# Two window tiles of the sample attention in other places, and their first loads on another queue

## The chip, the cores and the metric

The kernel runs on one core of one Trainium2 chip. Its time is the device time of one execution in microseconds (us); the profile is of one execution too. Five engines work side by side, each in its own order: PE (matrix products, and turning tiles over through a product with the identity; PEld is its weight load), DVE (vector operations, and 32x32 block transposes), ACT (activations and copies), POOL (element-wise work, and requests to transfer data) and SP (requests only). Transfers (DMA) go between the large memory and the on-chip memory of 128 partitions, SBUF. PE writes its results to eight accumulator banks, PSUM, from which DVE and ACT fetch them.

## The reference

One inference step of a decoder layer for a prompt of 512 tokens and eight sample sequences of eight tokens, each of these with 2048 cached tokens. Two attentions stand beside each other: FoX, over all tokens with a forgetting bias, and NSA, with three parts (compressed blocks, selected blocks, a window of 512). Then gates, an output projection and an MLP follow. What matters here is the sample sequences' attention:

```python
fox_all = jnp.concatenate([gather_pages(fox_pool, page_table), pm['fox_rows']], axis=1)
o_fox = fox_attend(pm['fox_q'], cf[:, past:], pos[past:], fox_all[:, :, 0], fox_all[:, :, 1], cf, pos)
nsa_all = jnp.concatenate([gather_pages(nsa_pool, page_table), pm['nsa_rows']], axis=1)
win_all = jnp.concatenate([win_buf, pm['win_rows']], axis=1)
o_nsa = nsa_attend(pm['nsa_q'], pos[past:], pm['nsa_gate'], kc, vc, c_end, ks_blk, vs_blk,
                   win_all[:, :, 0], win_all[:, :, 1], w_pos)
```

For each sequence 2 MB of FoX rows, 2 MB of selected-block rows and 512 KB of window rows are read.

## The kernel before, in words

**Stages.** A first stage sums the compressed blocks; then come projections, the prompt's attention (until about 427 us), the sample sequences' attention (about 422 to 545), the mixing of the branches with the output projection, and the MLP.

**The sample stage** (`sample_attention`) walks the eight sequences b = 0 to 7. Three pairs of rooms, each room 16 KB per partition, hold the rows in turn: `fr` for FoX and `sr` for the selected blocks. Pair 0 (fr0, sr0) and pair 1 (fr1, sr1) are tiles of their own; pair 2 lies in `room2`, which the prompt's attention uses until its end. A piece is a quarter of a room; `sample_fox(b, i, eng)` asks for FoX piece i of sequence b in one transfer of 512 KB, `sample_page(b, i, eng)` for the NSA piece in four transfers of 128 KB, one per page, whose numbers the queue first loads from the page table (L162). All go through `dma` (L151), which fixes their order on the queue as written. Window rows come in one transfer of 512 KB per sequence into `wr0` (even b) or `wr1` (odd b), by `window_load` (L1615).

For each sequence, PE forms scores (`ss`, L77, from rows that DVE has turned in `key_turn`, L1809), the last of them from two small tiles, `W2` and `CT`, which ACT fills by copies. DVE adds a ramp and takes the maxima (L1828, into `zF`; for the new tokens L1843, and L1851 for the new tokens of the window), ACT takes exponentials of `sN` and `zF`, PE turns them (`spn`, then sixteen `sp`), ACT copies these to `spT` and `zK`, and PE multiplies them with the rows (`so`). Only when `so` has read a piece may the next sequence but two be loaded there. The window goes by pairs of sequences: `window_keys` (L1908) turns wr's keys on PE (`wk`) and ACT copies them to `wkt`; `window_scores` (`sw`) uses both tiles of a pair. For the first pair, `window_keys(0)` and `window_keys(1)` stand ahead of `turn_weights(0)`, so that PE's order is wk of sequence 0, wk of sequence 1, spn, sp, so, sw, ss of sequence 1.

**What sets the order.** PE's order is the order of the program here (`link`, L87, chains each product to the one before). For the other engines a planner, which runs the program against its own idea of the times, sets the order unless `issue_after` fixes it. Requests of SP and POOL take eight semaphores each in turn, so a queue issues a transfer only when the one eight before it on that queue has landed.

**Places in SBUF.** Pools are opened and closed like a stack. A tile takes the bytes that follow the tile before it, and at its first write waits for the last use of each earlier tile that had any of these bytes. The pool `spw` lies over the prompt stage's buffers. Per partition, from its start:

| tile | bytes | what lay there in the prompt stage, latest first |
|---|---|---|
| D3b | 0 to 2047 | factors of the last FoX heads (Ffox3, ffox3) |
| CT | 2048 to 4095 | ffox3, Ffox1 |
| W2 | 4096 to 8191 | ffox2, Ffox1, early tiles |
| wr0 | 8192 to 12287 | compressed-block tiles cS, cP, cT |
| wkt, two tiles | 12288 to 16383 | cT, PTfox300, PTfox310 |
| wr1 | 16384 to 20479 | PTfox310, PTfox302, PTfox301 |

The buffers of the prompt stage there are: one of 2048 bytes that ends at 895 (Ffox3), one from 896 (ffox3), two from 2944 on (Ffox1, then ffox2), cpos, triS and first cS (7040 to 9087), later cS, cP and cT (to 13183), and four of 2048 from 13184 on (PTfox300, PTfox310, PTfox302, PTfox301). PTfox are turned weights of the last prompt heads, which PE reads in its last `ofox` products; Ffox1 is read by DVE in `oT<-ofox,Ffox` of the second FoX head, ffox2 by PE in `fcfox` of the third.

**Requests ahead of the loop** (L1650 to L1663): SP asks in the written order for sequence 1, with wr0 ahead of FoX piece 3, and then for sequence 2. POOL copies a part of D3b (L1657), prepares keys of sequence 1 (`key_prep`), asks for pages 0 and 2 of sequence 2, then for wr1, and prepares keys of sequence 2.

Of the kernel before, what the change touches and what calls it, by code (L numbers as in the profile page):

```python
# [6 lines left out]
F32 = mybir.dt.float32  # L7
# [7 lines left out]
P = 128  # L15
# [30 lines left out]
class Step:  # L46
# [1573 lines left out]
    def sample_attention(self, sp, ctx):  # L1620
# [11 lines left out]
        maps = [t(f"map{x}", [P, n]) for x, n in enumerate((2, 2, 2, 4))]  # L1632
        pw = self.pool("spw", ctx)
        self.D3.append(pw.tile([P, 16, 32], F32, name="D3b"))
        self.CT = pw.tile([P, 512], F32R, name="CT")
        self.W2 = pw.tile([P, NB, P], F32R, name="W2")
        w0 = pw.tile([P, 4, 256], F32, name="wr0")
        self.wkt = [pw.tile([P, 512], F32, name=f"wkt{x}") for x in range(2)]
        self.wrt = [w0, pw.tile([P, 4, 256], F32, name="wr1")]
        for b in range(3):  # L1640
            self.rows[b] = self.rooms[b]
        self.chain = ""
# [5 lines left out]
            self.key_counts(0)  # L1648
            self.act(self.CT, self.ct)
        page, fox = self.sample_page, self.sample_fox  # L1650
        for ask, b, i in ((fox, 1, 0), (fox, 1, 1), (page, 1, 0), (fox, 1, 2), (page, 1, 1), (fox, 1, 3), (page, 1, 2), (fox, 2, 0),
                          (page, 1, 3), (fox, 2, 1), (fox, 2, 2), (fox, 2, 3), (page, 2, 1), (page, 2, 3)):
            if (b, i) == (1, 3) and ask == fox:
                self.window_load(0, "sync")
            ask(b, i, "sync")
        with self.tc.issue_after(self.issued["gpsimd"]):
            self.nc.gpsimd.tensor_copy(self.D3[1][:, :, 16:32], self.D3[0][:, :, 16:32])  # L1657
        self.key_prep(1)
        for i in (0, 2):
            page(2, i, "gpsimd")  # L1660
        self.window_load(1, "gpsimd")
        self.key_prep(2)
        last = NB - 1  # L1663

# [1074 lines left out]
```

## Time and profile before

| what | us |
|---|---|
| median of three runs | 1149.46 (1149.41 to 1152.69) |
| the profiled execution | 1152.17 |
| its span, first to last instruction | 1150.5 |
| PE busy in the span | 1086.0 |
| DVE busy | 821.0 |
| ACT busy | 544.5 |
| POOL busy | 230.5 |

Times in the views count from the span's start. In a timeline row stand the start, the length, the engine (PEld is the weight load, SPq the queue of SP), the line of the kernel, the operation, output and inputs by the names of the program (without numbers), sizes, and in brackets the idle time before it with what ended it; "issue" is a wait for nothing that the profile shows. Neighbours that are alike are merged to one row with a count. A row of the windows view has: the stretch, its length, the busy time of PE, PEld, DVE, ACT and POOL with their numbers of instructions, the granted clock of PE as a share, the busy share of the DMA engines, and GB/s. A row of the waits view has the waiting engine and operation, who ended the wait, and the total, the number and the longest of these waits.

### The profile page before, as it was taken

What the parts mean: (1) busy time and instruction counts of PE and PEld (TensorE: products, weight loads), DVE (VectorE), ACT (ScalarE), POOL (GpSimd) and SP (SyncE); (2) the same over time, 40 slices, a digit from 0 to 9 for tenths busy, and PEclk for the clock granted to TensorE, in tenths of its full rate; (3) what the DMA queues carried; (4) which work ended last, traced back from release to release, by engine and by line L of the source; (5) the groups of instructions that cost most, each with busy time, mean ns of one, the idle gap of its engine ahead of it and who ended that gap; (6) DMA issues with size and microseconds to landing.
All of it is one profiled execution on the core that took longest, in us unless ns stands there. A gap on an engine that the chain in (4) does not pass through costs nothing.

```text
span 1150.5 us, 24616 instructions
## 1 busy us (share of the span) xinstructions
PE 1086.0 (94%) x9089; PEld 937.6 (81%) x9089; DVE 821.0 (71%) x2011; ACT 544.5 (47%) x1146; POOL 230.5 (20%) x320
## 2 busy tenths in 40 slices
PE   3899999999999995789999999999999999999998
PEld 3897789988666654556999999998989989899896
DVE  5898666685788865766987757769657658475668
ACT  3466643444777754456644435372514324143230
POOL 6540000002211513441000000012312122321202
PEclk9899999999999997999999999999999999999999
DMA  8997585764786797996643364252313224132242
GB/s 197 294 287 212 195 275 149 246 215 135 254 269 208 214 283 229 349 337 197 179 103 86 88 196 126 72 169 72 111 37 111 74 73 140 44 111 69 61 118 84
DMA packets 169049, 191.75 MB, mean 167 GB/s; under 512 B 17849, under 2 KB 147330, under 8 KB 166754
## 3 DMA queue, kind: packets, MB, share of 16 engines
q1 hardware_dynamic: 154674, 151.52, 44.7%
q0 software_dynamic: 12080, 37.62, 9.9%
q8 instruction: 71, 1.16, 0.4%
q10 hardware_dynamic: 2176, 1.05, 0.4%
q14 instruction: 48, 0.39, 0.1%
HBM read 179.89 MB, written 31.16 MB: 183 GB/s over the span
## 4 chain that ended last, share of the span: by engine, by line
PE 80%; DVE 7%; DMA 5%; ACT 3%; issue 3%; SPq 2%; POOL 0%; POOLq 0%; DVEq 0%; ACTq 0%
PE dn L77 18%; PE hid L77 6%; PE z L77 5%; PE br L77 4%; PE wo L77 4%; PE up L77 4%; PE upx L77 3%; PE upv L77 3%; DMA winr<-in_w_in 3%; PE mg L77 2%; PE ss L77 2%; SPq L155 2%; PE so L77 2%; PE mgv L77 2%; PE mgx L77 2%
## 5 line engine op out<-in xcount | busy, mean ns | idle before, releaser
L100 DVE TENSOR_TENSOR acc<-acc,dn 128x512 f32<-128x512 f32 x66 | 44.3, 684 | 54.0 <-PE dn L77 53.9
L77 PE MATMUL hid<-xh,w1hlk 128*128 128x256 f32 (+1 forms) x192 | 47.6, 341 | 16.8 <-ACT xh L112 16.8
L77 PE MATMUL z<-winh,h2r 128*128 128x264 f32 (+1 forms) x288 | 57.3, 288 | 2.3 <-ACT adw L112 2.3
L77 PE MATMUL z<-winh,h 128*128 128x264 f32 (+1 forms) x288 | 55.8, 284 | 0.0
L112 ACT ACTIVATE xh<-cpg 128x512 fp32r<-128x512 f32 x64 | 37.6, 623 | 36.2 <-PE hid L77 22.3
L112 ACT ACTIVATE u<-c 128x512 fp32r<-128x512 f32 x64 | 24.1, 434 | 59.2 <-PE dn L77 45.3
L77 PE MATMUL hid<-xh,w1hlv 128*128 128x256 f32 (+1 forms) x192 | 47.9, 341 | 3.9 <-ACT w1hlv L112 2.4
L131 DVE TENSOR_TENSOR xl<-cpg,xh 128x512 fp32r<-128x512 f32 x64 | 42.3, 682 | 11.6 <-ACT xh L112 11.5
L77 PEld LDWEIGHTS hid<-xh,w1hlk 128*128 128x128 f32 x192 | 33.3, 202 | 20.7 <-ACT xh L112 17.0
L2403 POOL TENSOR_TENSOR wur<-wur 128x512 f32<-128x512 f32 x12 | 19.8, 1653 | 148.4 <-DVE wu1l L131 55.5
L77 PEld LDWEIGHTS z<-winh,h2r 128*128 128x128 f32 x288 | 45.6, 190 | 3.6 <-ACT adw L112 2.5
L77 PEld LDWEIGHTS z<-winh,h 128*128 128x128 f32 x288 | 45.8, 190 | 0.0
L77 PE MATMUL z<-winl,h 128*128 128x264 f32 (+1 forms) x160 | 44.5, 284 | 0.5 <-DVE winl L131 0.5
L470 DVE STREAM_TRANSPOSE cpg<-cpg 128x1024 f32<-128x1024 f32 (+1 forms) x36 | 39.2, 1109 | 7.3 <-DMA cpg<-in_cache_nsa_kv 7.2
L77 PE MATMUL z<-winl,h2r 128*128 128x264 f32 (+1 forms) x160 | 44.4, 284 | 0.0
L155 POOL DMA_DIRECT2D cpg<-in_cache_nsa_kv x72 | 37.7, 525 | 27.9 <-issue 12.3
L77 PEld LDWEIGHTS hid<-xh,w1hlv 128*128 128x128 f32 x192 | 33.6, 202 | 8.0 <-ACT w1hlv L112 2.6
L77 PE MATMUL br<-oL,wbh 128*128 128x288 f32 x128 | 37.7, 295 | 0.0
L77 PE MATMUL br<-oH,wbl 128*128 128x288 f32 x128 | 37.7, 295 | 0.0
L77 PE MATMUL br<-oH,wbh 128*128 128x288 f32 x128 | 37.7, 294 | 0.0
L1828 DVE CUSTOM_DVE_ANT_1 zF<-ss,scr 128x512 f32<-128x512 f32 x32 | 20.2, 687 | 20.5 <-PE ss L77 20.5
L131 DVE TENSOR_TENSOR winl<-winr,winh 128x1056 fp32r<-128x1056 f32 (+1 forms) x16 | 19.6, 1234 | 18.7 <-ACT winh L112 18.6
(926 smaller groups left out, 3605.2 us busy)
## 6 DMA issues: line engine op xcount, KB each, us to landing
adw<-in_w_ada SPq DMA_DIRECT2D x16, 1024.0 KB
foxD<-in_cache_fox_kv SPq DMA_DIRECT2D x128, 128.0 KB
wur<-in_w_up SPq DMA_DIRECT2D x32, 512.0 KB
wdr<-in_w_down SPq DMA_DIRECT2D x32, 512.0 KB
wada<-in_w_ada SPq DMA_DIRECT2D x8, 1024.0 KB
sr<-in_cache_nsa_kv SPq DMA_DIRECT2D x64, 128.0 KB
cpg<-in_cache_nsa_kv SPq DMA_DIRECT2D x56, 128.0 KB
cpg<-in_cache_nsa_kv POOLq DMA_DIRECT2D x56, 128.0 KB, 5.7
```

Of the source, the lines that this page charges most:

```text
L77: ins = self.nc.tensor.matmul(out, a, b, start=start, stop=stop, skip_group_check=True)
L100: self.nc.vector.tensor_tensor(out, a, b, op=op)
L112: return self.nc.scalar.activation(out, in_, f, **kw)
L131: self.splits.append((eng or self.nc.vector).tensor_tensor(l, x, h.bitcast(F32), op=OP.subtract).ins)
L155: self.issued[eng] = getattr(self.nc, eng).dma_start(out, in_).ins
L470: self.flipped = self.nc.vector.transpose(v, v).ins
L1828: self.nc.vector.tensor_tensor_reduce(self.S[:, :, q, :], pbs[q].rearrange("p (c s) -> p c s", s=32), self.ramp[:, None, 32 * (q % 2):32 * ...
L2403: gp(a12, a12, a11, op=OP.subtract)
```

## The change

The two window tiles get other places in the pool, `wr1` behind an unused tile `edge` of 896 bytes; the other tiles of the pool shift with them. And both first window loads are asked for by SP: sequence 0's ahead of FoX piece 0 of sequence 1, and sequence 1's ahead of FoX piece 2, which now also stands ahead of page piece 0. POOL's request for wr1 is gone.

```diff
         self.D3.append(pw.tile([P, 16, 32], F32, name="D3b"))
+        pw.tile([P, 224], F32, name="edge")
+        w1 = pw.tile([P, 4, 256], F32, name="wr1")
         self.CT = pw.tile([P, 512], F32R, name="CT")
+        self.wrt = [pw.tile([P, 4, 256], F32, name="wr0"), w1]
         self.W2 = pw.tile([P, NB, P], F32R, name="W2")
-        w0 = pw.tile([P, 4, 256], F32, name="wr0")
         self.wkt = [pw.tile([P, 512], F32, name=f"wkt{x}") for x in range(2)]
-        self.wrt = [w0, pw.tile([P, 4, 256], F32, name="wr1")]
...
-        for ask, b, i in ((fox, 1, 0), (fox, 1, 1), (page, 1, 0), (fox, 1, 2), (page, 1, 1), (fox, 1, 3), (page, 1, 2), (fox, 2, 0),
+        for ask, b, i in ((fox, 1, 0), (fox, 1, 1), (fox, 1, 2), (page, 1, 0), (page, 1, 1), (fox, 1, 3), (page, 1, 2), (fox, 2, 0),
                           (page, 1, 3), (fox, 2, 1), (fox, 2, 2), (fox, 2, 3), (page, 2, 1), (page, 2, 3)):
-            if (b, i) == (1, 3) and ask == fox:
-                self.window_load(0, "sync")
+            if b == 1 and ask == fox and i in (0, 2):
+                self.window_load(i // 2, "sync")
             ask(b, i, "sync")
...
             page(2, i, "gpsimd")
-        self.window_load(1, "gpsimd")
         self.key_prep(2)
```

By the same stack of bytes the places after the change are:

| tile | bytes | what lay there in the prompt stage |
|---|---|---|
| D3b | 0 to 2047 | as before |
| edge | 2048 to 2943 | (never written) |
| wr1 | 2944 to 7039 | Ffox1, ffox2 |
| CT | 7040 to 9087 | cpos, triS, cS |
| wr0 | 9088 to 13183 | cS, cP, cT |
| W2 | 13184 to 17279 | PTfox300, PTfox310 |
| wkt, two tiles | 17280 to 21375 | PTfox302, PTfox301 |

## Prediction

> **What bounds the kernel now.** I read the views from the whole to the stage: page, chain of waits, windows, then one engine at a time around the longest wait.
>
> ```profile
> span 1150.5 us, 24616 instructions
> PE 80%; DVE 7%; DMA 5%; ACT 3%; issue 3%; SPq 2%; POOL 0%; POOLq 0%; DVEq 0%; ACTq 0%
> ```
>
> PE sets the end; what is not PE on the chain is where time can come from. The chain of waits over the start of the sample stage, in order of time (start, length, what):
>
> ```profile
> 425.36 1.45 PE ofox L77 x8
> ...
> 426.91 0.70 DVE oT L100
> ...
> 427.73 0.40 POOL D3b L1657
> ...
> 429.51 5.17 DMA room<-in_cache_nsa_kv
> ...
> 437.02 6.02 DMA wr<-in_state_win_kv
> 443.03 0.14 issue
> 443.17 1.09 PE wk L83 x4
> 444.26 0.21 PE spn L83
> 444.47 3.33 PE sp L83 x16
> 447.81 1.03 PE so L77 x64
> ```
>
> The chain leaves PE at 426.8, goes through DVE's last prompt product to POOL's D3b (L1657), POOL's eight page requests for sequence 2, and only then to wr1, the second sequence's window rows (L1661), which land at 443.03. PE and ACT, with the stage's rows by window:
>
> ```profile
> 429.78 0.66 PE L83 MATMUL wk<-identF,wr 128*128 128x128 f32 x4
> 443.17 1.09 PE L83 MATMUL wk<-identF,wr 128*128 128x128 f32 x4 [12.74 <-DMA wr<-in_state_win_kv]
> ```
> ```profile
> 435.00:440.00 5.00, 0.00 (x0) 0.00 (x0) 3.05 (x7) 0.84 (x3) 1.28 (x3) 0.50 1.06 356
> 442.00:449.50 7.50, 6.33 (x89) 5.45 (x89) 0.00 (x0) 3.66 (x7) 0.57 (x1) 0.63 0.06 15
> 450.00:470.00 20.00, 16.48 (x434) 10.15 (x419) 16.83 (x63) 9.27 (x21) 11.00 (x22) 1.00 0.97 333
> ```
>
> The reader is to see three things. PE turned wr0's keys at 429.78 and then stood 12.74 us for wr1, with nothing else to do, since its order is written out. Its clock (third column from the right) fell to 0.50. And the transfers (share, last but one) were full until about 442, empty to 449.5, and full again: the idle PE held back the rooms into which sequence 3's rows go.
>
> **The change, part by part.** It has three: places, requests on SP, one request less on POOL.
>
> *Places.* The tiles of the old stage are laid one behind the other, so the sizes in the code give who lay there. wr1 moves from the room of PTfox302, PTfox301 and the end of PTfox310 (read by PE until 426.8, the 425.36 row) to that of Ffox1 and ffox2 exactly, the `edge` tile of 896 bytes being what makes it exact. wr0 goes over cS, cP and cT buffers; CT over cpos, triS and cS; W2 over PTfox300 and PTfox310; wkt, first written behind 430, over PTfox302 and PTfox301. The last uses:
>
> ```profile
> 411.92 0.61 PE L83 MATMUL fcfox<-identF,ffox 128*128 128x128 f32 x4
> 423.32 1.07 PE L77 MATMUL ofox<-PTfox,zK 128*64 128x512 f32 x4
> 428.96 0.51 PE L77 MATMUL ss<-CT,W 32*128 32x512 f32 x4
> ```
> ```profile
> 410.42 0.69 DVE L100 TENSOR_TENSOR oT<-ofox,Ffox 128x512 f32<-128x512 f32 x1
> ```
> ```profile
> L77 PE MATMUL oc<-cT,pvc x16: 587/613/638, 298.8 to 360.6; 32*64 32x512 f32 x16
> ```
>
> wr1's new place is free at 412.5 (411.92 + 0.61; Ffox1 at 411.1), wr0's since about 361. W2 is the one tile that gets a later release: 423.32 + 1.07 = 424.4. ACT's copies to W2 and CT:
>
> ```profile
> 422.65 1.06 ACT L112 ACTIVATE W<-scr 128x1024 fp32r<-128x1024 f32 x1
> 423.60 0.63 ACT L112 ACTIVATE CT<-oT 128x512 fp32r<-128x512 f32 x1
> 432.66 0.35 ACT L112 ACTIVATE sN<-sN,ss 128x64 f32<-128x64 f32 x1 [8.43 <-DVE ss L1858]
> 434.14 1.13 ACT L112 ACTIVATE zF<-zF,ss 128x1024 f32<-128x1024 f32 x1
> 435.27 0.57 ACT L112 ACTIVATE wkt<-wk 128x512 f32<-128x512 f32 x1
> 444.36 0.60 ACT L112 ACTIVATE wkt<-wk 128x512 f32<-128x512 f32 x1 [8.51 <-PE wk L83]
> ```
>
> W2 then ends at 425.5 and CT, queued behind it, at 426.1; PE wants both at 428.96, and ACT has nothing else before 432.66. Cost nothing, cover 2.9 us; even a release with the last ofox at 426.8 gives 426.8 + 1.06 + 0.63 = 428.5.
>
> *Requests on SP.* SP's requests now:
>
> ```profile
> 403.56 2.68 SPq L155 DMA_DIRECT2D scr<-qD  x4
> 412.04 0.81 SPq L155 DMA_DIRECT2D fr<-foxD  x2
> ...
> 420.11 0.42 SPq L155 DMA_DIRECT2D wr<-in_state_win_kv  x1
> ...
> 424.49 2.30 SPq L155 DMA_DIRECT2D sr<-in_cache_nsa_kv  x4
> ```
>
> wr0 goes out at 406.3 (403.56 + 2.68), in SP's idle time before 412.04; wr1 behind the two fr rows at 412.9, just after its place is free. Nothing stands queued behind a wait. Issue costs 0.42 each; half a megabyte at the 356 GB/s of the window row is 0.524/356 = 1.5 us of transfer. SP asks at most eight ahead of what has landed, so its later requests slip with the transfers. The rows of sequence 1 behind both slip 1.5 us for the last of them (wr0 stood ahead of these before, only wr1 is new), 2.9 us for the first. Both window tiles land well before PE's 429.78. DVE turns sequence 1's rows here, and sequence 2's at 455.90:
>
> ```profile
> 432.08 0.22 DVE L1851 CUSTOM_DVE_ANT_0 scr<-sn,scr 128x64 f32<-128x64 f32 x1
> 436.77 1.28 DVE L1809 STREAM_TRANSPOSE sr<-sr 128x512 f32<-128x512 f32 x2
> 455.90 2.48 DVE L1809 STREAM_TRANSPOSE room<-room 128x512 f32<-128x512 f32 x4
> ```
>
> Had they landed only when DVE took them, the last turn would end at 438.1 + 1.5 = 439.6, and PE reaches the scores of sequence 1 only after its first so, behind 440.6 (below). So nothing; without that cover it would cost the 1.5. Sequence 2's rows are the end of the same bytes, which moved as a whole within the full stretch: still by 443, wanted at 455.90 - 8.2 = 447.7.
>
> *POOL.* It loses the request that stood behind D3b and the eight pages; these keep their places. What it did behind wr1, preparing the second next sequence's keys, comes earlier and frees nothing that anyone waits for.
>
> *What is late next.* With wr1 there, PE's keys of sequence 1 need a bank that DVE's L1851 frees at 432.3: they run 432.3 to 433.0. spn needs the bank of wr0's keys, which ACT copies behind its exponentials, 435.27 to 435.84. A hand-over is 0.14 (the 443.03 row), so spn runs at 436.0 for 0.21 and sp from 436.2. Of the sp group two prices stand in the trace: 3.33 at clock 0.50, and at full clock
>
> ```profile
> 457.65 2.23 PE L83 MATMUL sp<-identF,zF 128*128 128x128 f32 x16 [0.17 <-ACT zF L112]
> 483.88 0.32 PE L77 MATMUL so<-room,zK 128*32 128x64 f32 x7 [1.70 <-issue]
> ```
> ```profile
> 485.00:486.00 1.00, 1.00 (x28) 0.74 (x26) 1.00 (x3) 0.96 (x2) 0.68 (x2) 0.57 0.67 163
> ```
>
> I take 3.33: the clock also fell at 485 after a pause of only 1.7 us, and here PE works 0.7 us between 430.4 and 436.0. So the first so starts at 436.2 + 3.33 = 439.6, rounded up, in place of 447.81: **8.2 us**; at full clock 9.4.
>
> The Trainium skill, "TensorE: Matmul & The Clock Gate", section "HAM oscillation — how this bites in real kernels", says that only pauses over about 3.4 us throttle. By it the two pauses left, 1.9 and 2.9 us, would keep the full clock, and the gain be 9.4. The 485 row speaks against it.
>
> *Does it last?* From so onward the loop repeats; its rows are asked for as rooms come free. The transfers were 0.94 idle in 442 to 449.5, 7.0 us; closing that gap brings all later rows 7.0 earlier, with compute 8.2 earlier, so they need 1.2 us of slack. In 440 to 560:
>
> ```profile
> DVE zF L1828 <- PE ss L77: 18.6, 6, 5.2
> ```
> ```profile
> PE so L77 <- issue: 7.2, 6, 2.3
> ```
>
> DVE, which takes the rows first, waits for PE and not for transfers, so the slack is there. The mixing stage behind shifts whole: its tiles that take these places wait in both layouts for the last reads of the window rows.
>
> Sum: -8.2 us. The profiled execution took 1152.17 (span 1150.5), the median of the runs is 1149.46; the profiled one would come to 1144.0, the median to **1141.3**.
>
> **Rivals.**
> - *Copy brought forward.* The planner, which lays ACT's order, now sees wr0 early and may put the copy of its keys ahead of the exponentials; ACT is idle until 432.66. Then spn runs at 433.1, sp as the exponentials finish (434.14, 435.27), 4 groups to 437.5 at half clock: so 10.3 earlier, 1139.2. For it: the idle ACT; against: rows must then have 3.3 us of slack.
> - *Given back.* PE's waits in so with no visible releaser (7.2 us in six, 1.2 each) fall where transfers are full, none in 442 to 449.5. That stretch is now full too: one or two more, and the 1.2 us of slack missing, leave 8.2 - 3.6 = 4.6: 1144.9.
> - *It doesn't do it.* If wr1's new place were held longer (say to DVE's 427.6), SP would stand there 14.7 us with the rows of sequence 1 behind it: last request 426.8 + 14.7 = 441.5, landed 5.2 later (the 429.51 row) and turned in 1.3, 448.0. Scores of sequence 1 begin now after so (1.03) and as much again for sw, 449.9; 1.9 us remain: 1147.6.
> - *Slower.* The same unseen waits, at 438 to 530, grow because the queues never run empty. They cost 1.2 us each; the sign turns at 8.2/1.2 = 7 additional ones, more than doubling the present six; at nine it is 1149.5 - 8.2 + 10.8 = 1152.1. The row of six speaks against: the load behind them (0.97) hardly rises.
>
> **How the numbers follow.** Forecast 0.42; brought forward 0.27; given back 0.18; not done 0.07; slower 0.06. A measurement here tells apart about 0.3%, 3.4 us. The first three are faster, 0.87; "it doesn't do it" is within, 0.07; slower 0.06. The range takes the first three with their bounds: full clock with the copy brought forward, 10.3 + 1.1, gives 1138.1, and the transfers bring at most some tenths more, so 1137.7; upward, 1144.9 and two further waits of 1.2: 1147.3.
>
> **What would show it.** Right: the 12.74 us before the second wk is gone and that group starts near 432.3; wr issued twice by SP near 406 and 413 without a wait; the first so near 439.6 (437.5 if the copy came forward); no empty transfers in 442 to 449.5; W and CT end before 428.9. Wrong: SP idle before wr, an ss that waits for a DMA, or PE waits without releaser in so beyond ten.

## The result, and the profile after

| | kernel before | changed kernel |
|---|---|---|
| median of 20 runs each | 1152.72 us | 1146.69 us |
| lowest and highest | 1146.91, 1161.92 | 1142.14, 1152.07 |
| ratio, with its 95% interval | 1 | 0.9943 [0.9921, 0.9965] |
| profiled execution: time, span | 1152.17, 1150.5 us | 1145.33, 1143.6 us |

The change makes the kernel faster, by 0.57% (0.35 to 0.79), some 6.6 us by this ratio; the medians differ by 6.0. The forecast was 8.2 us, a ratio of 0.993. Its time of 1141.3 us lies 5.4 us below the measured median: 3.3 us of that come from the start (the three runs shown before had a median of 1149.46 us, twenty have 1152.72), the other 2.1 from the gain (8.2 less 6.0). So the median stands only 0.6 us below the upper end of the range, 1147.3.

The page of the changed kernel: its span, and the shares of the chain by engine.

```profile
span 1143.6 us, 24614 instructions
...
PE 74%; DVE 10%; DMA 6%; ACT 4%; issue 3%; SPq 2%; POOL 1%; DVEq 0%; ACTq 0%; POOLq 0%
```

The chain of waits of the changed kernel over the start of the sample stage (start, length, what):

```profile
424.85 1.07 PE ofox L77 x7
...
432.17 1.14 ACT zF L112 x2
433.35 3.67 PE sp L83 x16
437.03 1.87 PE so L77 x64
438.89 1.18 PE sw L77 x4
440.10 0.69 DVE scr L1919
...
443.02 0.62 DVE sr L1809
443.69 2.69 PE ss L77 x52
```

No DMA and no POOL stands in this part of it any more. Where the chain before went from POOL's copy over eight page requests to wr1, it now goes through ACT's exponentials to PE's sp. The first so starts at 437.03 in place of 447.81. But 0.9 us of these 10.8 lie ahead of the stage: the last prompt product (ofox) ends at 425.92 in place of 426.81. This end moved between 424.1 and 430.0 us over the ten profiled executions of the study, so all distances below are counted **from the end of the last ofox**. By that measure the first so comes at 11.1 in place of 21.0, that is 9.9 us earlier. Then, at 440.10, the chain changes to DVE, and that is new; the second experiment looks there.

The order of time on SP, ACT and PE in the changed kernel:

```profile
404.52 0.45 SPq L155 DMA_DIRECT2D wr<-in_state_win_kv  x1
411.17 0.81 SPq L155 DMA_DIRECT2D fr<-foxD  x2
412.14 0.34 SPq L155 DMA_DIRECT2D wr<-in_state_win_kv  x1
```
```profile
423.55 1.06 ACT L112 ACTIVATE W<-scr 128x1024 fp32r<-128x1024 f32 x1 [1.66 <-PE ofox L77]
424.51 0.61 ACT L112 ACTIVATE CT<-oT 128x512 fp32r<-128x512 f32 x1
429.59 0.60 ACT L112 ACTIVATE wkt<-wk 128x512 f32<-128x512 f32 x1 [4.46 <-PE wk L83]
431.73 0.35 ACT L112 ACTIVATE sN<-sN,ss 128x64 f32<-128x64 f32 x1 [1.54 <-DVE ss L1858]
```
```profile
428.08 0.50 PE L77 MATMUL ss<-CT,W 32*128 32x512 f32 x4
428.89 0.66 PE L83 MATMUL wk<-identF,wr 128*128 128x128 f32 x4
431.53 0.63 PE L83 MATMUL wk<-identF,wr 128*128 128x128 f32 x4 [1.98 <-issue]
...
433.35 3.67 PE L83 MATMUL sp<-identF,zF 128*128 128x128 f32 x16 [0.79 <-ACT zF L112]
```

SP asks for both window tiles without a wait. W is now held for 1.66 us by PE's read of its new place, and still ends with CT at 425.12, 2.96 us before PE takes them at 428.08. The third row of ACT is the surprise: the copy of wr0's keys (wkt) stands ahead of the exponentials, where in the kernel before it stood behind them. The stretches that the prediction showed, in the changed kernel (third column from the right: granted clock; last but one: share of the transfers):

```profile
435.00:440.00 5.00, 5.00 (x81) 3.64 (x80) 1.60 (x4) 2.74 (x6) 1.10 (x2) 0.58 1.05 354
442.00:449.50 7.50, 5.38 (x146) 2.99 (x150) 5.10 (x21) 0.88 (x4) 1.78 (x4) 1.00 0.77 253
450.00:470.00 20.00, 16.96 (x346) 11.41 (x347) 15.33 (x43) 11.48 (x24) 11.19 (x22) 0.91 1.01 359
```

PE is busy all of 435 to 440, yet at a clock of 0.58; the hole in the transfers, 0.06 before, is filled to 0.77. PE's waits in the changed kernel from 420 to 560 (what waited for what: us in total, times, longest):

```profile
PE so L77 <- issue: 7.2, 6, 2.2
PE ss L77 <- DVE sr L1809: 2.6, 1, 2.6
```

The 12.74 us are gone; 1.98 us are left before the second wk, where the prediction had 1.9. The second row is what is new.

### The profile page after: what moved, and what is told of

Same layout as the page of the kernel before. It is cut to its first block, busy times and chain, and to the rows that moved or that the text cites. A ratio compares the mean times of both kernels' runs of the same rounds, so it can differ in the third digit from the quotient of the medians.

```text
span 1143.6 us, 24614 instructions
## 1 busy us (share of the span) xinstructions
PE 1086.8 (95%) x9089; PEld 937.3 (82%) x9089; DVE 820.2 (72%) x2011; ACT 544.2 (48%) x1146; POOL 229.8 (20%) x319
## 4 chain that ended last, share of the span: by engine, by line
PE 74%; DVE 10%; DMA 6%; ACT 4%; issue 3%; SPq 2%; POOL 1%; DVEq 0%; ACTq 0%; POOLq 0%
PE dn L77 16%; PE hid L77 5%; PE z L77 5%; PE br L77 4%; PE wo L77 4%; PE upv L77 3%; PE upx L77 3%; PE ss L77 3%; PE mg L77 2%; DMA winr<-in_w_in 2%; SPq L155 2%; PE so L77 2%; PE mgv L77 2%; PE mgx L77 2%; PE upz L77 2%
## 5 line engine op out<-in xcount | busy, mean ns | idle before, releaser
L131 DVE TENSOR_TENSOR xl<-cpg,xh 128x512 fp32r<-128x512 f32 x64 | 42.3, 682 | 10.1 <-ACT xh L112 10.1
L1828 DVE CUSTOM_DVE_ANT_1 zF<-ss,scr 128x512 f32<-128x512 f32 x32 | 20.2, 687 | 20.2 <-PE ss L77 20.2
```

The lines of the kernel that those rows point to most:

```text
L131: self.splits.append((eng or self.nc.vector).tensor_tensor(l, x, h.bitcast(F32), op=OP.subtract).ins)
L1828: self.nc.vector.tensor_tensor_reduce(self.S[:, :, q, :], pbs[q].rearrange("p (c s) -> p c s", s=32), self.ramp[:, None, 32 * (q % 2):32 * ...
```

## The experiments

Times of one execution say little here: the 20 runs of the kernel before spread over 15 us. So each kernel is read by its own trace, counted from the end of its last ofox: when the first so starts, when the mixing stage starts (first mg), and how long PE stood in so without a visible releaser between 420 and 560. PE has such waits in sp, ss and accS too, behind the first so; the column "net" is the first mg less all of them. It is a rough measure, since a wait on PE may hide another, and it differs by up to 1.3 us between two traces of one kernel.

| kernel | first so | first mg | so, no releaser | net | ratio to the kernel before |
|---|---|---|---|---|---|
| before | 21.0 | 116.2 | 7.2 | 105.7 | 1 |
| places alone | 20.3 | 117.0 | 10.1 | 104.3 | one execution |
| requests alone | 11.1 | 114.3 | 8.4 | 105.5 | one execution |
| changed | 11.1 | 109.6 | 7.2 | 99.6 | 0.9943 [0.9921, 0.9965] |
| changed, again | 10.8 | 112.9 | 9.8 | 100.9 | 0.9955 [0.9929, 0.9981] |
| copy behind | 12.9 | 112.8 | 9.7 | 101.2 | one execution |
| wr1 alone moved far ahead | 12.9 | 107.9 | 5.7 | 99.8 | one execution |
| turn first | 11.1 | 108.1 | 8.2 | 97.5 | 0.9894 [0.9869, 0.9919] |
| turn first, again | 11.1 | 105.9 | 7.5 | 97.8 | 0.9904 [0.9869, 0.9940] |
| turn first and PE kept busy | 9.7 | 103.9 | 4.9, and 3.5 in accS | 95.5 | 0.9903 [0.9868, 0.9939] |

From the first mg to the end of the span all ten need 607.5 to 610.2 us, in no order that follows the changes: the mixing stage and all behind it shift as a whole.

### Places alone, requests alone

First the requests of the kernel before, in the layout of the changed kernel (against the changed kernel, as all diffs here):

```diff
-        for ask, b, i in ((fox, 1, 0), (fox, 1, 1), (fox, 1, 2), (page, 1, 0), (page, 1, 1), (fox, 1, 3), (page, 1, 2), (fox, 2, 0),
+        for ask, b, i in ((fox, 1, 0), (fox, 1, 1), (page, 1, 0), (fox, 1, 2), (page, 1, 1), (fox, 1, 3), (page, 1, 2), (fox, 2, 0),
...
-            if b == 1 and ask == fox and i in (0, 2):
-                self.window_load(i // 2, "sync")
+            if (b, i) == (1, 3) and ask == fox:
+                self.window_load(0, "sync")
...
             page(2, i, "gpsimd")
+        self.window_load(1, "gpsimd")
```

> The changed kernel's places with the requests of the kernel before: wr0 ahead of the fourth prompt-part row of sequence 1, wr1 behind POOL's eight page requests. If the queue and not the room held wr1 (prediction's reading: D3b's copy, then eight pages, then wr1): wr1 goes out at 436 to 438 as before, PE waits 11 to 13 us for it, first so at 447 to 448, span within 1 us of the kernel before profiled beside it. If the room held it: wr1 lands 5 us or more earlier, and most of the gain is here.

With the room free early and the request still in POOL's queue, where it goes out at 433.48 behind the eight page requests, PE waits as before:

```profile
PE wk L83 <- DMA wr<-in_state_win_kv: 12.3, 1, 12.3
```

The new room alone brings next to nothing: the first so comes 0.7 us earlier, the first mg does not, and net of the waits it is 1.4 us earlier, about as much as two traces of one kernel differ. The other half, the changed kernel's requests in the layout of the kernel before:

```diff
-        pw.tile([P, 224], F32, name="edge")
-        w1 = pw.tile([P, 4, 256], F32, name="wr1")
...
-        self.wrt = [pw.tile([P, 4, 256], F32, name="wr0"), w1]
+        w0 = pw.tile([P, 4, 256], F32, name="wr0")
+        self.wrt = [w0, pw.tile([P, 4, 256], F32, name="wr1")]
```

> The requests of the changed kernel with the places of the kernel before: wr1 asked for by SP ahead of the second sequence's rows, but into the old room, which PE reads until its last prompt product (426 to 427). If the room binds as the prediction said of its rival (it doesn't do it): SP stands at wr1 for some 13 to 14 us with the rows of sequence 1 behind it, these land at 446 to 447, the scores of sequence 1 start near 450, and the span is within 2 us of the kernel before. If the order of requests alone is enough: SP does not wait, first so below 439.

SP, then DVE of this kernel in order of time:

```profile
409.81 0.81 SPq L155 DMA_DIRECT2D fr<-foxD  x2
424.44 0.34 SPq L155 DMA_DIRECT2D wr<-in_state_win_kv  x1
```
```profile
440.50 0.65 DVE L1918 CUSTOM_DVE_ANT_0 scr<-sw,scr 128x512 f32<-128x512 f32 x1
444.24 0.71 DVE L1808 STREAM_TRANSPOSE sr<-sr 128x512 f32<-128x512 f32 x1 [0.46 <-DMA sr<-in_cache_nsa_kv]
```

SP stands from 410.62 to 424.44, 13.8 us, with the rows of sequence 1 behind it, as the prediction's rival had it for the new room. wr1 itself still comes in time (first so at 11.1), so the two cases of the expectation don't exclude each other: the wait has moved from wr1 to the rows. The last of them is turned only by 444.95, and PE stands 4.8 us for it. At the first mg 1.9 us of gain are left (116.2 less 114.3), the figure that the rival had worked out, but it is luck that the two agree: in this one execution the waits without a releaser are shorter, and net of them 0.2 us are left (105.7 less 105.5). **The room alone and the request alone bring little or nothing without the other.**

### The turn first: where 2.6 us went

The PE row "ss waits for DVE's sr" was read in DVE's order of time in the changed kernel:

```profile
435.93 0.67 DVE L1809 STREAM_TRANSPOSE sr<-sr 128x512 f32<-128x512 f32 x1
440.10 0.69 DVE L1919 CUSTOM_DVE_ANT_0 scr<-sw,scr 128x512 f32<-128x512 f32 x1 [3.50 <-PE sw L77]
...
442.94 0.69 DVE L1809 STREAM_TRANSPOSE sr<-sr 128x512 f32<-128x512 f32 x1
```

DVE stands 3.50 us for PE's window scores (sw), takes their maximum (L1919), builds the maps, and only then turns the last of sequence 1's rows, for which PE's scores wait. In the kernel before all these turns stood ahead of L1919. The order is the planner's; no line of the change names it. The experiment holds L1919 behind the last turn. In DVE's order nothing else moves in the sample stage until 490 us; behind that the planner also lays two small operations at the end of a sequence (at 495.6 in the changed kernel) and some of the mixing stage's work on DVE and ACT in another order. From the first mg to the end this kernel needs 610.2 and 607.6 us in its two executions, the changed one 608.1 and 609.3, so no gain is seen there:

```diff
-                self.nc.vector.transpose(v, v)
+                self.last_turn = self.nc.vector.transpose(v, v).ins
...
-        self.nc.vector.tensor_tensor_reduce(self.SWt[:, 0:512], pb, self.rw, 1.0, LOW, OP.add, OP.max, self.wst[i][:, 0:1])
+        with self.tc.issue_after(self.last_turn) if i == 0 else nullcontext():
+            self.nc.vector.tensor_tensor_reduce(self.SWt[:, 0:512], pb, self.rw, 1.0, LOW, OP.add, OP.max, self.wst[i][:, 0:1])
```

> The changed kernel, with DVE's maximum over the first window scores (L1919) held behind the last turn of sequence 1's rows; nothing else differs. Theory A (in the changed kernel the scores of sequence 1 wait 2.6 us because DVE's new order puts that turn, at 442.94, behind the maximum over scores that PE had not yet made, while the rows had landed at 432.07): PE's wait of 2.6 us in ss for DVE's sr goes, the last turn of sr ends before 441, the second part of ss starts near 441.1 instead of 443.69, and all behind comes up to 2.6 us earlier: ratio to the kernel before 0.9943 - 0.0023 = about 0.992. Theory B (the rows themselves came late, because the window rows went ahead of them on SP): the wait of 2.6 us stays, now with the maximum behind it, ratio 0.994. Theory C (the transfers of the loop behind bind anyway): the 2.6 us goes at ss of sequence 1 and comes back as waits for DMA or for rows by sequence 4, ratio 0.994.

DVE's last turns, and PE from sp to the scores behind the window scores, in this kernel:

```profile
434.94 1.26 DVE L1809 STREAM_TRANSPOSE sr<-sr 128x512 f32<-128x512 f32 x2
```
```profile
432.36 3.68 PE L83 MATMUL sp<-identF,zF 128*128 128x128 f32 x16 [0.61 <-ACT zF L112]
...
437.69 1.08 PE L77 MATMUL sw<-wkt,bdN 128*64 128x512 f32 x4
438.70 0.66 PE L77 MATMUL ss<-fr,scr 32*32 32x512 f32 x8
```

The last two turns run at 434.94 without a wait for a DMA, so the rows were there: not the transfers, DVE's order made PE wait. The wait is gone, the ratio is 0.9894 in place of 0.9943, and no wait for a DMA has taken its place: theory A holds, B and C don't. The same kernel was run again, beside the changed kernel on one chip:

> The kernel with the turn first once more, beside the changed kernel on the same chip. Theory A: 2 to 3 us below the changed kernel (2.6 from the wait, and what a later meeting with the instruction fetches gives or takes). Theory C: no difference.

> The changed kernel once more, as the measure for its neighbours on this chip: ratio to the kernel before 0.992 to 0.9965, the wait of 2.6 us in ss for sr there again, since it is in the order of DVE and not in the transfers; PE's waits without a releaser in so again five to seven, of other lengths than the first time if they are meetings with instruction fetches.

Medians 1143.11 us (7 runs) against 1149.26 us (12 runs), ratios 0.9904 and 0.9955 to the kernel before. The wait for sr is in the changed kernel again, 2.6 us, and in neither trace of the other. The medians differ by 6.1 us, more than the 2 to 3 expected. The gap is 0.5% both times, and in the first pair of comparisons the intervals don't overlap, while in the second they overlap. It is more than 2.6 us, 0.23%; but the intervals reach 0.2 to 0.35% to each side, so the size is not told apart from that. By the traces it is 1.5 us (109.6 less 108.1) to 7.0 us (112.9 less 105.9) at the first mg; net of the waits without a releaser, 2.1 (99.6 less 97.5) and 3.1 (100.9 less 97.8), close to the wait that is gone. This kernel beats both the one before and the changed one.

### The copy's place

The copy of sequence 0's keys held behind the exponentials (that of sequence 1 stands behind them in every kernel):

```diff
-        self.last_weights = self.act(self.wkt[b % 2], tb).ins
+        with self.tc.issue_after(self.last_exp) if b == 0 else nullcontext():
+            self.last_weights = self.act(self.wkt[b % 2], tb).ins
```

> The changed kernel, with ACT's two copies of the first pair's keys (wkt) held behind the exponentials of sequence 1, the order that the prediction assumed. If the copy's place is what brought the stage 10.8 us forward in place of 8.2: spn behind ACT's copy, at about 435 to 436, first so 438.0 to 439.6 (the changed kernel 437.03), that is 1 to 2.5 us later, and the end later by no more than that, since PE then waits less for sr. If ACT's order does not matter there: so at 437.0 as before.

The chain of waits with the copy held behind the exponentials:

```profile
434.99 2.26 ACT zF L112 x4
437.25 0.49 ACT wkt L112
...
438.21 3.41 PE sp L83 x16
441.62 1.11 PE so L77 x64
```

The last ofox ends at 428.75 here, so the first so comes at 12.9 in place of 11.1: the copy's place is worth 1.8 us. 21.0 less 12.9 is 8.1: with the order of ACT that the prediction assumed, its step comes out to a tenth. Holding the copy also put DVE's turns ahead of the maximum again (the last two start at 438.75, the maximum at 443.79), so here the wait for sr is gone, and the expectation that the end comes later by 1 to 2.5 us can't be judged from this one execution, with its 9.7 us of waits in so; net of such waits its first mg is 0.3 to 1.6 us later than in the two of the changed kernel.

Then wr1 alone moved far ahead, and wr0 left where it stood before:

```diff
-            if b == 1 and ask == fox and i in (0, 2):
-                self.window_load(i // 2, "sync")
+            if b == 1 and ask == fox and i in (2, 3):
+                self.window_load(3 - i, "sync")
```

> The changed kernel, with the two requests in other places on SP: wr1 ahead of the third prompt-part row of sequence 1, wr0 where it stood in the kernel before, one request later. If only the second tile's way out of POOL's queue matters: wr1 lands before 425, no wait of 12.7 us, first so within 3 us of the changed kernel's 437.03. If wr0's earlier request carries part of it: PE's first wk later than 430 and so beyond 440. If DVE's order is what costs 2.6 us at ss, that wait is there or gone with the place of the last sr turn in that order, not with the landing of the rows.

The chain of waits of this kernel:

```profile
431.66 2.27 ACT zF L112 x4
433.92 0.49 ACT wkt L112
...
434.88 3.41 PE sp L83 x16
438.30 1.33 PE so L77 x64
```

With wr0 asked for as late as before, the planner leaves the copy behind the exponentials and DVE's turns ahead of L1919: first so at 12.9, no wait for sr, first mg at 107.9. So wr0's earlier request is what changed both orders in the changed kernel: it won 1.8 us on ACT and lost 2.6 us on DVE. DVE's order seems to follow the copy's place, since holding the copy, with wr0 early, brought DVE's old order back too. The request of wr1, into its new room, is what the gain comes from: net of the waits without a releaser this kernel's first mg is at 99.8, beside 99.6 and 100.9 for the changed one.

### The clock in the two pauses

In the changed kernel sp runs at a low clock behind two pauses of PE, 1.98 and 0.79 us. This experiment takes the kernel with the turn first and fills its two pauses (1.98 and 0.61 us) with products that nobody reads (lines added to that kernel):

```diff
                 for o in range(2):
                     self.window_keys(o)
+                    if o == 0:
+                        self.warm(12)
...
         self.act(self.TN, tb[:NS, 0:P])
+        if b == 0:
+            self.warm(5)
...
+    def warm(self, n):
+        for j in range(n):
+            self.tr(self.acc[:, 0:P], self.identF)
```

> The kernel with the turn first, and in it 17 transposes of the unit matrix added that nobody reads (12 between the two wk groups, 5 between spn and sp, into the bank of accS, which is written anew later): PE is kept busy through the two pauses ahead of sp. It computes the same. Theory D (sp and the first so are slow because the clock falls in these pauses, whose longest is 2 us): granted clock 1.00 from 430 to 440, sp in 2.2 to 2.6 instead of 3.68, first so and the 64 behind it in 1.03 instead of 1.73, the window scores about 2 us earlier against the end of the prompt's last ofox, ratio 0.9894 - 0.0017 = about 0.988. Theory E (sp is slow because its operands come late from ACT, whose second exponential ends 1 us into it): sp stays at 3 us or more although the clock is full, and nothing is gained. If the full clock needs a longer busy stretch than these 17 give: clock still below 0.8 in sp, no gain.

PE in order of time, and the window of sp of the same kernel:

```profile
430.74 1.47 PE L83 MATMUL accS<-identF 128*128 128x128 f32 x12
432.89 0.63 PE L83 MATMUL wk<-identF,wr 128*128 128x128 f32 x4 [0.67 <-issue]
...
433.71 0.71 PE L83 MATMUL accS<-identF 128*128 128x128 f32 x5
434.71 2.23 PE L83 MATMUL sp<-identF,zF 128*128 128x128 f32 x16 [0.29 <-ACT zF L112]
```
```profile
432.40:436.00 3.60, 2.72 (x19) 2.05 (x20) 3.57 (x15) 2.92 (x7) 2.90 (x6) 1.00 1.02 393
```

With no pause over 0.7 us left the clock stays at 1.00, sp takes 2.23 us in place of 3.68, and the first so comes 1.35 us earlier, at 9.7. Theory D is shown for sp. In the whole time nothing of it can be seen (1143.03 us against 1143.11 beside it, both intervals 0.7% wide): the trace has a gain at the first mg, 103.9 against 105.9 and 108.1, and the times can't tell 1.4 us apart.

## Why the prediction was right, and where it was wrong

- **The bound** was right: wr1 in POOL's queue. With the room alone changed, the wait is 12.3 us.
- **The places** cost nothing, as said; the cover of W and CT is 2.96 us (2.9 forecast).
- **The requests on SP** went out at 404.52 and 412.14 without a wait. That wr1's room must be free for it is shown by the kernel with the requests alone: SP stands 13.8 us there, where the rival "it doesn't do it" had 14.7, and most of the gain is gone (its 1.9 us at the first mg were met by luck, as said above).
- **What is late next** was right in its mechanism and its size: 8.1 us where ACT's order is the one assumed, against 8.2. That order did not stay. The rival "copy brought forward" is what happened, with 9.9 us at the first so against its 10.3. The half clock that the step took was right (3.67 for sp, clock 0.58); that the so and sw behind it may run slow too, 1.87 and 1.18 in place of 1.03 each, was missed. They did so in the profiled execution; in the other one of the changed kernel both took 1.03.
- **The step that failed** is the one on sequence 1's rows: "Had they landed only when DVE took them, the last turn would end at 438.1 + 1.5 = 439.6 ... So nothing". It asked when the rows land and took DVE's order as given. The rows were in time; the turn was put behind work that waits for PE, and ended at 443.63. That took 2.6 us, more than the 1.8 us that the same planner had won on ACT. The prediction let the planner move ACT's order, in a rival, and not DVE's.
- **Does it last?** Right in the main. With the turn first, the 9.9 us of the first so are still 8.1 and 10.3 at the first mg, and 8.2 and 7.9 net of the waits without a releaser. DVE's longest waits there are for PE (L1828 for ss, 18.3 us in the changed kernel from 435 to 560), none for a transfer, so the rows had the slack.
- **Given back and slower**: the waits in so without a releaser are 7.2 us in six, as before; and 9.8, again in six, in another execution of the same kernel. They did not grow in number, and their sum differs by 2.6 us between these two executions of one kernel. That they fall where transfers are full is as far as the prediction went; the last section has more on their cause.
- **The sum**: 9.9 us at the first so (8.1, and 1.8 for the copy); 1.0 lost in so and sw, which run at a low clock in this execution; 3.2 lost in the scores of sequence 1, which take 7.4 us to the so behind them in place of 4.1, 2.6 of it the wait for the turn. That leaves 5.7 us behind these scores; the times say 6.6 us (4.0 to 9.1), and at the first mg the two executions of the changed kernel show 6.6 and 3.3, and 6.1 and 4.8 net of the waits without a releaser. That the forecast of 8.2 came near is in part luck: a gain that it had only as a rival (1.8) and two losses that it did not have (1.0 and 3.2) partly met.

The Trainium skill, "TensorE: Matmul & The Clock Gate", section "HAM oscillation — how this bites in real kernels", has only pauses above about 3.4 us throttle. The measurement differs: pauses of 1.98 and 0.79 us came before a clock of 0.58 here, and filling them brought 1.00.

## What to carry to other kernels

Where a planner lays the order of an engine, price a change with that order free on every engine that the moved transfers feed, not only with durations: look, on each, for an instruction that something waits for and that may now be put behind one that itself waits. A tile that comes late needs both its room and its place in a queue; test the two halves apart, since either alone may bring nothing. And when executions of the same kernel differ by more than the change, count from a fixed event close ahead of it in each trace, and compare also without the waits that no engine and no data transfer explains.

## What the runs showed of the hardware

The clock fell after shorter pauses than expected, also in the middle of the loop. In the first run of the kernel with the turn first, PE stood 2.16 us in a so without a releaser, and the mixing products behind it ran at half clock (windows of that kernel, then PE in order of time):

```profile
530.00:533.00 3.00, 0.86 (x45) 0.75 (x45) 2.66 (x4) 2.97 (x7) 0.45 (x1) 1.00 0.58 168
533.00:536.40 3.40, 3.40 (x22) 3.33 (x15) 3.12 (x6) 3.40 (x6) 1.36 (x3) 0.51 0.79 243
```
```profile
532.13 0.24 PE L77 MATMUL so<-fr,zK 128*32 128x64 f32 x1 [2.16 <-issue]
...
533.71 0.44 PE L77 MATMUL mg<-hH,wmh 128*128 128x288 f32 x1
```

In the kernel with wr1 alone moved, PE stood 0.69 us at the same place, and mg ran at full speed:

```profile
532.39 0.22 PE L77 MATMUL so<-fr,zK 128*32 128x64 f32 x1 [0.69 <-issue]
...
533.69 0.29 PE L77 MATMUL mg<-hH,wmh 128*128 128x288 f32 x1
```

So the longer wait cost twice: its own 2.16 us, and some 1.5 us behind it (14 mg matmuls started 0.24 us apart in place of 0.13).

The length of a pause alone does not decide. In the changed kernel PE's wait of 2.62 us for the turn left the clock at 1.00 (the row of 442 to 449.5 above), while 1.70 us in the kernel before were followed by 0.57. And a stretch at half clock has a fixed length: in all ten traces each one between 420 and 560 us lasts 3.4 us, or two or four times that. The pauses ahead of sp, 1.98 and 0.79 or 0.83 us, brought 6.8 us of it in the profiled execution of the changed kernel (432.3 to 439.2) and 3.4 us in the other (436.9 to 440.3). What places these stretches was not tried.

The waits in so without a releaser were not tried either, but the traces say something of them. The page of each kernel lists the transfers by queue; in the changed kernel two queues bring instructions, and one of them, in packets of 16 KB, has this row (packets, MB, share of the 16 engines):

```profile
q8 instruction: 71, 1.16, 0.4%
```

PE and its weight loads have 18178 of the 24614 instructions, so this is taken to be PE's queue. Of the 54 waits in so without a releaser that are longer than 0.25 us (ten traces, 420 to 560 us), 53 end 2.25 to 2.75 us after such a packet starts, and one 4.1 us after it, whose packet took 2.5 us in place of about 1.1; in the changed kernel one starts at 459.21, and the wait of 2.24 us ends at 461.77. Of the 14 to 16 packets between 14 and 110 us behind the last ofox, only some are followed by a wait. So PE seems to have run out of instructions there; no experiment shows it. These waits stand mostly at the same places of the program: counted from the last ofox, five of the six in the one execution of the changed kernel have a partner within 0.5 us in the other, at 35.8, 51.2, 63.0, 68.8 and 75.5. Their lengths vary, one can be missing or added (3.17 us just ahead of the first mg in the other execution), and their sum in so ran from 4.9 to 10.1 us.
